# Seven-product units at the start of the second halves' pairs, with their sums prepared in the mixers, and a plain unit's pieces held in program order behind them

## The chip, the cores and the metric

The kernel runs on one core of a Trainium2 chip. The metric is the time of the device for one execution in microseconds; 2365.54 us is the median of three runs (2365.01 to 2366.05).

## The reference

Two layers act on 256 tokens of width D = 2048, in float32. Layer 0 mixes tokens with a bidirectional mLSTM, layer 1 with a bidirectional HGRN2 recurrence; each mixer is followed by a gated MLP with a width-3 depthwise convolution, and a last RMSNorm closes the trunk. The change touches the matrix products behind the mixers and in the gated MLP:

```python
def conv_glu(hn, w_up, conv_w, conv_b, w_down):
    u = hn @ w_up
    a, v = jnp.split(u, 2, axis=-1)          # each 256 x 5504
    ...
    return (jax.nn.gelu(c, approximate=False) * v) @ w_down

for layer in range(DEPTH):
    ...
    h = h + mix
    h = h + conv_glu(rmsnorm(h, norm_ffn_g[layer]), ...)
return rmsnorm(h, final_g)
```

## The kernel before

**Weights.** All weights stream from HBM in the order of use. Each loaded tile `raw` is split into a high part wh (a cast on ScalarE, L147) and a low part wl (a subtraction on VectorE, L148); activations are split likewise. A product of two blocks is then three matmuls: high by high, high by low, low by high. A generator yields the split pieces (128 x 1024 or 128 x 512) and runs a few pieces ahead of TensorE.

**The gated MLP** of a layer is done in two halves of its inner width, 22 and 21 K-tiles of 128. A half consists of an up phase (L365 and L369, TensorE computes u for its K-tiles, then convolution, gelu and product) and two *pairs*. A pair multiplies the half's K-tiles by two column blocks of 512 of w_down and adds the result into hm, which holds the residual stream. The mixers' output projections have one such pair each, over 16 K-tiles.

**Units.** A pair takes its K-tiles by twos. Such a unit is a product of 2 x 2 by 2 x 2 blocks (two token halves, two K-tiles, two column blocks). A *plain* unit does the eight block products, 24 matmuls of 128x512, into four banks C11 to C22 (named pc in the profile), from two pieces of 1024 columns. A *seven-product* unit does seven products, 21 matmuls, partly into four other banks P1, P6, P7, P5 (named mm), with differences of weights and of activations as operands. It needs pieces of 1024, 1024, 1024 and 512 columns. Its activation sums sx are made by `token_sums` (L579 to L581) in the up phase. Its weight sums come from VectorE in one of two ways: *on the fly* in `combine` (four subtractions, L207), or *prepared*: `prepare` loads the unit's 1 MB, makes four subtractions of 128x512 (L646) and stores 1 MB to a scratch area in HBM, tscr; the pair later loads 768 KB of weights plus 1 MB of prepared blocks in place of 1 MB of weights. Preparation goes on in the mixers (through SyncE's queue, loads with L403, stores with L649) and in the up phases (through POOL's queue, L407). After the last seven-product unit of a pair, `mid` (L593 to L604) adds the banks P1 to P5 into hm: a ScalarE copy L596, VectorE adds L597 to L602, POOL adds L603 and L604. At a pair's end `done` (L610) adds the C banks.

**The tables.** SEVEN names the seven-product units of each layer's halves, FLY those made on the fly, FIRST how many of the first half's first pair are prepared in the mixer, SPLIT how the second pair of the second half is shared between mixer, first up phase and second up phase. `prepare_early` is given the start and the period of the preparation in the mixer.

**Order.** Operations are written by the generators and then put in order for each engine by a scheduler, with the exception of those that are wrapped in `pin` (kept in the order of the program). Side jobs such as `prepare` and `token_sums` are stepped by a clock of estimated costs.

**The end.** The last pair's last three units are done token half by token half (`ending`, L245 to L270). In the second token half the block C22 is computed in two parts of 256 columns, the latter into a bank named rest. `FinalNorm.half` (L515 to L544) adds the banks, squares, sums, takes the power on POOL (L534), scales and stores.

## Time and profile before

| | |
|---|---|
| median of 3 runs | 2365.54 us |
| profiled execution | 2365.45 us, its span 2363.7 us |
| TensorE busy | 2352.0 us (100%) |
| VectorE busy | 2012.2 us (85%) |
| ScalarE busy | 1478.2 us (63%) |
| POOL busy | 309.1 us (13%) |
| DMA | 656.06 MB, mean 278 GB/s |
| chain that ended last | TensorE 98%, VectorE 1% |
| granted TensorE clock | 0.999 of full speed |

The page's span runs from the first to the last instruction. Its times are microseconds. In a timeline a row begins with its start and its length; xN joins N instructions; what stands in brackets is the idle time ahead of it and what ended it. "pc<-wh,g" is a matmul that writes bank pc from weights wh and activations g. TensorE's matmuls are pipelined, so that the modelled end of one lies behind the start of the next. The halves of layer 0's MLP have their pairs at about 634 to 742 us and 974 to 1080 us, those of layer 1 at about 1910 to 2018 us and 2250 to 2356 us.

### The profile page before, as it was taken

The numbers are of one execution on the slowest core, as the hardware profiler recorded it, in microseconds if no ns is written. First come the engines' busy times: TensorE is split into PE (matmuls) and PEld (weight loads), VectorE is DVE, ScalarE is ACT, GpSimd is POOL, SyncE is SP. The second block draws the span as 40 slices with busy tenths as digits, with TensorE's granted clock in tenths as the row PEclk, the third lists the DMA queues.
The fourth block names the chain that finished last, engine by engine and source line by source line (L and its number), as shares of the span: only waits on it lengthen the run. The fifth ranks groups of instructions, "written<-read, shape, count | busy, mean of one in ns | idle before, by whom it ended". The sixth has DMA issues, their size and how long they took to land.

```text
span 2363.7 us, 38636 instructions
## 1 busy us (share of the span) xinstructions
PE 2352.0 (100%) x14533; PEld 2013.4 (85%) x14533; DVE 2012.2 (85%) x3123; ACT 1478.2 (63%) x2352; POOL 309.1 (13%) x460
## 2 busy tenths in 40 slices
PE   9999999999999999999999999999999999999998
PEld 7888888888888888888888888888888888888887
DVE  7777787999998999897888788788799989899888
ACT  7655456555665555676777777766555577555565
POOL 0100001111000111000232322220011100111100
PEclk9999999999999999999999999999999999999999
DMA  8776756899898999886656666566799999799985
GB/s 303 239 245 244 239 204 216 292 337 338 308 358 312 311 334 332 290 316 228 212 203 222 214 220 209 206 207 234 247 329 338 319 336 362 272 332 327 333 328 205
DMA packets 129180, 656.06 MB, mean 278 GB/s; under 512 B 14544, under 2 KB 15696, under 8 KB 85600
## 3 DMA queue, kind: packets, MB, share of 16 engines
q1 hardware_dynamic: 96192, 536.32, 64.3%
q0 software_dynamic: 32224, 116.47, 13.8%
q8 instruction: 114, 1.87, 0.3%
q10 hardware_dynamic: 576, 0.79, 0.1%
q14 instruction: 74, 0.61, 0.1%
HBM read 576.92 MB, written 76.61 MB: 276 GB/s over the span
## 4 chain that ended last, share of the span: by engine, by line
PE 98%; DVE 1%; issue 0%; DMA 0%; ACT 0%; POOL 0%; SPq 0%; POOLq 0%; DVEq 0%
PE mm L365 37%; PE mm L369 19%; PE mm L381 18%; PE pc L236 11%; PE mm L236 9%; PE pn L865 1%; PE py L1124 1%; DVE wl L148 0%; PE pd L1074 0%; PE pa L1074 0%; PE pz L446 0%; DMA raw<-in_w_first 0%; PE S L851 0%; PE pz L1145 0%; PE pa L1099 0%
## 5 line engine op out<-in xcount | busy, mean ns | idle before, releaser
L365 PE MATMUL mm<-xt,wh 128*128 128x512 f32 x3776 | 1312.6, 394 | 0.2 <-issue 0.2
L148 DVE TENSOR_TENSOR wl<-raw,wh 128x1024 fp32r<-128x1024 f32 (+1 forms) x844 | 1034.2, 1232 | 230.4 <-ACT wh L147 223.2
L147 ACT CAST wh<-raw 128x1024 fp32r<-128x1024 f32 (+1 forms) x844 | 874.9, 1043 | 545.5 <-PE mm L365 346.6
L369 PE MATMUL mm<-xt,wl 128*128 128x256 f32 x3776 | 1043.6, 278 | 0.0
L365 PEld LDWEIGHTS mm<-xt,wh 128*128 128x128 f32 x3776 | 705.7, 188 | 160.9 <-issue 0.4
L369 PEld LDWEIGHTS mm<-xt,wl 128*128 128x128 f32 x3776 | 709.5, 188 | 4.8 <-issue 0.3
L381 PE MATMUL mm<-wh,xt 128*128 128x512 f32 x1024 | 324.1, 392 | 1.6 <-ACT wh L147 1.5
L236 PE MATMUL pc<-wh,g 128*128 128x512 f32 (+1 forms) x676 | 231.6, 388 | 0.0
L381 PEld LDWEIGHTS mm<-wh,xt 128*128 128x128 f32 x1024 | 190.9, 188 | 41.0 <-ACT wh L147 2.1
L646 DVE TENSOR_TENSOR praw<-praw 128x512 f32<-128x512 f32 x284 | 196.4, 692 | 14.6 <-DMA praw<-in_w_d 9.0
L381 PE MATMUL mm<-wl,xt 128*128 128x512 f32 x512 | 199.7, 391 | 0.0
L236 PE MATMUL mm<-wh,sx 128*128 128x512 f32 x456 | 160.1, 389 | 0.0
L147 ACT CAST wh<-T 128x512 fp32r<-128x512 f32 (+1 forms) x152 | 124.5, 835 | 46.8 <-PE pc L236 19.5
L148 DVE TENSOR_TENSOR wl<-T,wh 128x1024 fp32r<-128x1024 f32 (+1 forms) x152 | 142.4, 959 | 12.5 <-ACT wh L147 11.9
L236 PEld LDWEIGHTS pc<-wh,g 128*128 128x128 f32 x676 | 126.7, 188 | 25.9
L236 PE MATMUL pc<-wl,g 128*128 128x512 f32 (+1 forms) x338 | 131.5, 389 | 0.6 <-DVE wl L148 0.5
L1214 ACT COPY avc<-mm 128x256 f32<-128x256 f32 x172 | 64.3, 374 | 87.9 <-PE mm L369 87.9
L381 PEld LDWEIGHTS mm<-wl,xt 128*128 128x128 f32 x512 | 96.2, 188 | 18.6
L407 POOL DMA_DIRECT2D praw<-in_w_d x108 | 57.7, 535 | 413.0 <-DMA tscr<-praw 408.4
L1087 DVE TENSOR_TENSOR QK<-QK,G 128x256 f32<-128x256 f32 x224 | 104.6, 515 | 5.0 <-ACT kq L1066 4.7
L236 PEld LDWEIGHTS mm<-wh,sx 128*128 128x128 f32 x456 | 85.6, 188 | 17.8
L1066 ACT COPY kq<-QK 128x512 f32<-128x512 f32 x112 | 74.5, 670 | 41.2 <-DVE QK L1087 35.1
(248 smaller groups left out, 2337.5 us busy)
## 6 DMA issues: line engine op xcount, KB each, us to landing
raw<-in_w_up SPq DMA_DIRECT2D x172, 1024.0 KB, 7.7
praw<-in_w_d POOLq DMA_DIRECT2D x108, 512.0 KB, 6.8
tscr<-praw POOLq DMA_DIRECT2D x108, 512.0 KB, 8.7
T<-tscr SPq DMA_DIRECT2D x71, 768.0 KB, 7.2
raw<-in_w_d SPq DMA_DIRECT2D x68, 768.0 KB, 6.7
raw<-in_w_bq SPq DMA_DIRECT2D x48, 1024.0 KB, 5.0
raw<-in_w_ao SPq DMA_DIRECT2D x24, 1024.0 KB, 4.8
raw<-tscr SPq DMA_DIRECT2D x71, 256.0 KB, 7.0
```

Of the source, the lines that this page charges most:

```text
L147: pin(act.copy(wh[:, :m], r))
L148: pin(dve.tensor_tensor(wl[:, :m], r, wh[:, :m].bitcast(F32), ALU.subtract))
L236: pin(pe.matmul(ps, a, b, start=bank not in begun, stop=stop and i == 2))
L365: hold(pe.matmul(ps[f], wh[:, c:c + P], x, start=k + kk == 0, stop=False))
L369: hold(pe.matmul(ps[f][:, 0:T], wl[:, c:c + P], x[:, 0:T], start=False, stop=k + kk == ch.nk - 1))
L381: pe.matmul(ps[t], x[:, a + t * P:a + (t + 1) * P], w[:, c], start=st and i == 0, stop=sp and i == 2)
L407: tc.keep_in_program_order(pool.dma_start(dst, src))
L646: hold(dve.tensor_tensor(out, x, y, ALU.subtract))
L865: pe.matmul(pn[:, 0:258], w, v, start=(i == 0), stop=(i == len(parts) - 1))
L1066: act.copy(m, blocks(QK, h))
L1087: dve.tensor_tensor(two[:, j], two[:, j], by[:, j], ALU.mult)
L1214: act.copy(z, p[:, T:2 * T])
```

## The change

Both pairs of both second halves get unit 0 as a seven-product unit (layer 0: units 0 to 8 for 1 to 8; layer 1: 0 to 7 for 1 to 7). Layer 0's unit 5 is made on the fly in the second half's first pair only, and prepared in its second pair. Of the first halves' first pairs, nine and ten units are prepared in the mixers instead of seven; the second pair's shares are (0, 3, 6) and (0, 4, 4) instead of (0, 1, 6) twice. So 12 and 13 units are prepared in the mixers for 10 and 10, 14 and 14 in the first up phases as before, 14 and 12 in the second for 13 and 13. The mixers' preparation starts sooner and steps faster. The pieces of a plain unit right behind a seven-product unit are held in program order, as are `mid`'s first copy and first add. In the final norm, the add of C22 takes 256 columns in the second token half.

```diff
@@ -47,10 +47,10 @@
 LEAD = 48
 TEMP = 3
 GATES = 4 * AH
-SEVEN = (range(10), range(1, 9)), (range(10), range(1, 8))
-FLY = (), (5,), (), ()
-FIRST = 7
-SPLIT = (0, 1, 6), (0, 1, 6)
+SEVEN = (range(10), range(9)), (range(10), range(8))
+FLY = ((), ()), ((5,), ()), ((), ()), ((), ())
+FIRST = 9, 10
+SPLIT = (0, 3, 6), (0, 4, 4)
 END = 3
 SCRATCH = 4096
 SEVEN_MIX = (2, 4, 6)
@@ -209,13 +209,14 @@
 
         for u in range(units):
             r = raw(u)
-            yield *parts(r[:, 0:1024], 1024, more=ch.pool), 1
+            hold = pin if u - 1 in ch.seven and u not in ch.seven else lambda ins: ins
+            yield *parts(r[:, 0:1024], 1024, hold, ch.pool), 1
             if u + 1 in ch.seven and u + 1 not in ch.stored:
                 combine(u + 1)
             if u in ch.seven:
                 yield *parts(kept[u][:, 0:1024], 1024, more=ch.pool), 1
             if 2 * u + 1 < ch.nk:
-                yield *parts(r[:, 1024:2048], 1024, more=ch.pool), 1
+                yield *parts(r[:, 1024:2048], 1024, hold, ch.pool), 1
             if u in ch.seven:
                 yield *parts(kept[u][:, 1024:1536], 512, more=ch.pool), 1
 
@@ -274,6 +275,7 @@
         alone = max(set(range(units)) - set(ch.seven))
         for u in range(units):
             if ch.last and u == units - END:
+                assert id(C22) not in begun
                 ending(u)
                 held.pop()
                 return
@@ -522,8 +524,8 @@
             dve.tensor_scalar(rc, ss[:, 2:3], 1.0 / D, rc, ALU.mult, ALU.add)
             last = keep.tile([P, 512], F32, tag=f"xt{4 + t}", name="fl")
             h = hm[:, t, 1536:2048]
-            dve.tensor_tensor(h, h, ps[1], ALU.add)
             m = 256 if t else 512
+            dve.tensor_tensor(h[:, 0:m], h[:, 0:m], ps[1][:, 0:m], ALU.add)
             dve.scalar_tensor_tensor(last[:, 0:m], h[:, 0:m], 1.0 / D, h[:, 0:m], ALU.mult, ALU.mult, accum_out=ss[:, 3:4])
             dve.tensor_tensor(rc, rc, ss[:, 3:4], ALU.add)
             if t:
@@ -593,8 +595,8 @@
         def mid(ps):
             P1, P6, P7, P5 = ps
             u = ev.tile([P, 512], F32, tag="jk", bufs=1, name="u")
-            act.copy(u, P1)
-            dve.tensor_tensor(part(0, 0), part(0, 0), P1, ALU.add)
+            pin(act.copy(u, P1))
+            pin(dve.tensor_tensor(part(0, 0), part(0, 0), P1, ALU.add))
             dve.tensor_tensor(u, u, P6, ALU.add)
             dve.tensor_tensor(part(0, 1), part(0, 1), P5, ALU.add)
             dve.tensor_tensor(part(0, 1), part(0, 1), u, ALU.add)
@@ -947,7 +949,7 @@
                 norm.finish()
                 done_v(ps, note)
                 side.push(start(gs))
-                prepare_early(box["mp"], 0, 62.0, 25.0)
+                prepare_early(box["mp"], 0, 55.0, 19.0)
 
             last = {}
 
@@ -992,7 +994,7 @@
             mp = box["mp"] = stack.enter_context(tc.tile_pool(name="hg", bufs=1))
             box["lv"] = mp.tile([P, 2 * P], F32, name="lv")
             late(box["lv"][:, 0:FINE * QUAD], cst_d[:, C_LV:])
-            prepare_early(mp, 1, 30.0, 38.0)
+            prepare_early(mp, 1, 30.0, 27.0)
             box["turn"] = 0
             lb = box["lb"] = mp.tile([P, KT], F32, name="lb")
             oml = box["oml"] = mp.tile([P, KT], F32, name="oml")
@@ -1284,9 +1286,10 @@
 
             w0, w1 = w_d0[layer][:, f0 * 1024:(f0 + nf) * 1024], w_d3[layer] if part else w_d1[layer]
             fly = FLY[2 * layer + part]
-            n = len(seven) - len(fly)
-            chunks.append(two(w0, 0, nxt if part else None, seven, fly, (0, 0, n) if part else (FIRST, n - FIRST)))
-            chunks.append(two(w1, 2, nxt if part and not ending else None, seven, fly, SPLIT[layer] if part else (0, n)))
+            m, n = (len(seven) - len(f) for f in fly)
+            early_ = FIRST[layer]
+            chunks.append(two(w0, 0, nxt if part else None, seven, fly[0], (0, 0, m) if part else (early_, m - early_)))
+            chunks.append(two(w1, 2, nxt if part and not ending else None, seven, fly[1], SPLIT[layer] if part else (0, n)))
             if part:
                 chunks[-1].last = ending
                 if ending:
```

TensorE, at the start of the second half's first pair in layer 0, before (mm at L369 ends the up phase; g are activations, sx their sums):

```order
L369 MATMUL mm<-xt_3941,wl 128x256
L236 MATMUL pc<-wh,g_7398 128x512
L236 MATMUL pc<-wl,g_7398 128x512
L236 MATMUL pc<-wh,g_7398 128x512
L236 MATMUL pc<-wh,g_7506 128x512
L236 MATMUL pc<-wl,g_7506 128x512
```

and in the change:

```order
L371 MATMUL mm<-xt_3961,wl 128x256
L237 MATMUL mm<-wh,g_7418 128x512
L237 MATMUL mm<-wl,g_7418 128x512
L237 MATMUL mm<-wh,g_7418 128x512
L237 MATMUL pc<-wh,g_7418 128x512
L237 MATMUL pc<-wl,g_7418 128x512
L237 MATMUL pc<-wh,g_7418 128x512
L237 MATMUL mm<-wh,sx 128x512
```

The pair begins with the first product of a seven-product unit, into an mm bank, and not with the first of a plain one. Over the whole program the matmuls into pc fall by 60 and those into mm rise by 48.

VectorE at the end of the first half's second pair in layer 0, before:

```order
L148 TENSOR_TENSOR wl<-T,wh 128x512
L597 TENSOR_TENSOR hm<-hm,mm 128x512
L599 TENSOR_TENSOR hm<-hm,mm 128x512
L601 TENSOR_TENSOR hm<-hm,mm 128x512
L148 TENSOR_TENSOR wl<-raw,wh 128x1024
L598 TENSOR_TENSOR u<-u,mm 128x512
L148 TENSOR_TENSOR wl<-raw,wh 128x1024 x2
```

and in the change (its lines 599, 600, 601, 603 are lines 597, 598, 599, 601 of before):

```order
L148 TENSOR_TENSOR wl<-T,wh 128x512
L601 TENSOR_TENSOR hm<-hm,mm 128x512
L148 TENSOR_TENSOR wl<-raw,wh 128x1024
L603 TENSOR_TENSOR hm<-hm,mm 128x512
L148 TENSOR_TENSOR wl<-raw,wh 128x1024 x2
L599 TENSOR_TENSOR hm<-hm,mm 128x512
L600 TENSOR_TENSOR u<-u,mm 128x512
```

The rows "wl<-raw" are the plain unit 10's two pieces and then the next phase's first. The pieces moved ahead of three of the four adds.

VectorE at the very end, second token half, before:

```order
L525 TENSOR_TENSOR hm<-hm,pc 128x512
L522 TENSOR_SCALAR fss<-fss 128x1
L527 SCALAR_TENSOR_TENSOR fl,fss<-hm 128x256
L528 TENSOR_TENSOR fss<-fss 128x1
L531 TENSOR_TENSOR hm<-hm,rest 128x256
L532 SCALAR_TENSOR_TENSOR fl,fss<-hm 128x256
L533 TENSOR_TENSOR fss<-fss 128x1
```

and in the change (lines 524, 528, 529, 530, 533, 534, 535 are 522, 525, 527, 528, 531, 532, 533 of before):

```order
L524 TENSOR_SCALAR fss<-fss 128x1
L528 TENSOR_TENSOR hm<-hm,pc 128x256
L533 TENSOR_TENSOR hm<-hm,rest 128x256
L529 SCALAR_TENSOR_TENSOR fl,fss<-hm 128x256
L534 SCALAR_TENSOR_TENSOR fl,fss<-hm 128x256
L530 TENSOR_TENSOR fss<-fss 128x1
L535 TENSOR_TENSOR fss<-fss 128x1
```

The add of rest, which needs the last matmul, moved ahead of the first part's square and its sum.

## The prediction

> **What bounds the kernel now.** I read the page's first part, then the chain of waits, then TensorE's waits.
>
> ```profile
> PE 2352.0 (100%) x14533; PEld 2013.4 (85%) x14533; DVE 2012.2 (85%) x3123; ACT 1478.2 (63%) x2352; POOL 309.1 (13%) x460
> PE 98%; DVE 1%; issue 0%; DMA 0%; ACT 0%; POOL 0%; SPq 0%; POOLq 0%; DVEq 0%
> 974.81 5.45 PE pc L236 x24
> 323.20 10.88 PE pc L236 x48
> PE mm L381 <- ACT wh L147: 1.5, 2, 0.9
> PE pc L236 <- DVE wl L148: 0.8, 3, 0.3
> ```
>
> TensorE is busy for 2352.0 of 2363.7 us and carries 98% of the chain that ended last. So the time can fall in three ways only: fewer matmuls, fewer of the short waits in front of them, or a shorter end after the last one. VectorE at 85% is next; it makes the low halves (wl, L148) that TensorE reads, and its two waits of this kind are visible above. The profiled execution took 2365.45 us; the median of the runs shown is 2365.54, 0.09 above, and I add that at the end. What a measurement can tell from no change, 0.2%, is 4.73 us.
>
> **Twelve matmuls fewer.** Four pairs of column blocks get a seven-product unit where a plain one was: 7 products of 3 matmuls for 8 of 3, so 3 fewer each, 12 in all. The price of one is its spacing, not its duration. The two chain rows above give it: 24 matmuls in 5.45 us and 48 in 10.88, 0.227 us each. The mean duration of the same form stands in this group row:
>
> ```profile
> L236 PE MATMUL mm<-wh,sx 128*128 128x512 f32 x456 | 160.1, 389 | 0.0
> ```
>
> 389 ns is longer because neighbours overlap; by it twelve would be 4.67 us, the far bound. I take 12 x 0.227 = **-2.72**. The Trainium skill, page "TensorE: Matmul & The Clock Gate", section "Back-to-back issue gap", gives about 131 ns as the sustained spacing of matmuls with 512 columns; by it the twelve would be an estimated 1.57 us and the forecast 1.15 us later. The chain rows disagree with that page for this kernel's float32 operands (0.227), and I stay with the rows.
>
> **Two waits behind a seven-product unit.** At the end of each first half, second pair, plain unit 10 follows seven-product unit 9. TensorE and VectorE in layer 0, from the timeline:
>
> ```profile
> 732.81 0.69 DVE L597 TENSOR_TENSOR hm<-hm,mm 128x512 f32<-128x512 f32 x1 [0.94 <-ACT u L596]
> 734.17 0.69 DVE L599 TENSOR_TENSOR hm<-hm,mm 128x512 f32<-128x512 f32 x1 [0.68 <-PE mm L236]
> 734.78 0.68 DVE L601 TENSOR_TENSOR hm<-hm,mm 128x512 f32<-128x512 f32 x1
> 735.11 1.29 PE L236 MATMUL pc<-wh,g 128*128 128x512 f32 x5
> 735.37 1.22 DVE L148 TENSOR_TENSOR wl<-raw,wh 128x1024 fp32r<-128x1024 f32 x1
> 736.51 0.68 DVE L598 TENSOR_TENSOR u<-u,mm 128x512 f32<-128x512 f32 x1
> 736.65 0.50 PE L236 MATMUL pc<-wl,g 128*128 128x512 f32 x1 [0.25 <-DVE wl L148]
> 736.99 0.63 PE L236 MATMUL pc<-wh,g 128*128 128x512 f32 x2
> ...
> 737.68 0.63 PE L236 MATMUL pc<-wh,g 128*128 128x512 f32 x2
> 738.38 0.50 PE L236 MATMUL pc<-wl,g 128*128 128x512 f32 x1
> 738.72 0.39 PE L236 MATMUL pc<-wh,g 128*128 128x512 f32 x1
> ```
>
> Five matmuls from 735.11 should let the sixth start at 736.24; it starts at 736.65 (0.41 lost) and the next 0.34 later instead of 0.227 (0.11). Two from 737.68 should end at 738.13; the next starts at 738.38 (0.25), and the one after loses 0.11 again: 0.87 together. The cause is VectorE's order: L599 waits for TensorE, L601 follows it, and only then come unit 10's pieces. Layer 1 repeats it:
>
> ```profile
> 2011.14 1.29 PE L236 MATMUL pc<-wh,g 128*128 128x512 f32 x5
> 2012.68 0.50 PE L236 MATMUL pc<-wl,g 128*128 128x512 f32 x1 [0.25 <-DVE wl L148]
> ...
> 2013.71 0.63 PE L236 MATMUL pc<-wh,g 128*128 128x512 f32 x2
> 2014.41 0.50 PE L236 MATMUL pc<-wl,g 128*128 128x512 f32 x1
> ```
>
> In the change both pieces are held, and one add (layer 0) or none (layer 1) stands ahead of the first. Layer 0 by the durations above: the add may start 0.42 after the start of product P5's last matmul (733.75 to 734.17); add pitch 0.61 (734.17 to 734.78), piece pitch 1.14 (735.37 to 736.51). First piece ready at 0.42 + 0.61 + 1.14 = 2.2; TensorE needs it 14 matmuls later, 3.2. Second: 2.2 + 0.61 + 1.14 = 3.9 against 20 matmuls, 4.5. Both waits go: 2 x 0.87 = **-1.74**. Lower bound 0, if each only moves to the next piece. What is late instead are the adds L597 and L598; nobody needs them before the banks are reused, some 35 matmuls on.
>
> **The second halves' first units.** A seven-product unit wants pieces of 1024, 1024, 1024 and 512 columns from VectorE instead of two of 1024: 1.14 + 0.61 = 1.74 us more per pair, while TensorE takes 3 x 0.227 = 0.68 less. So each of the four pair starts presses VectorE by 2.42 us. The busy times by window (length, busy PE, PEld, DVE, ACT, POOL with counts, clock, DMA share, GB/s) are the first pairs of layer 0's halves, its second half's second pair, and layer 1's:
>
> ```profile
> 634.00:690.00 56.00, 56.00 (x250) 46.38 (x250) 51.10 (x57) 42.27 (x52) 3.54 (x2) 1.00 0.89 342
> 974.00:1028.00 54.00, 54.00 (x241) 44.51 (x240) 49.33 (x58) 38.53 (x47) 3.46 (x2) 1.00 0.85 308
> 1028.00:1080.00 52.00, 52.00 (x239) 43.09 (x237) 48.47 (x54) 37.76 (x50) 2.57 (x2) 1.00 0.70 240
> 2250.00:2300.00 50.00, 50.00 (x224) 41.46 (x223) 42.94 (x50) 34.00 (x42) 3.47 (x2) 1.00 0.90 330
> 984.00:994.00 10.00, 10.00 (x46) 8.29 (x45) 10.00 (x12) 7.33 (x8) 0.00 (x0) 1.00 0.72 238
> ```
>
> Layer 0's first half already begins with a seven-product unit and TensorE is busy for 56.00 of its 56.00 us, so the cheap bound is 0. Its second half is fuller: 984 to 994 VectorE is busy all the time (unit 5's sums are made on the fly there). The first pair goes from 49.33 to 51.07 of 53.3 us, 96%; the second from 48.47 + 1.74, less four on-the-fly subtractions of 0.61, to 47.8 of 51.3, 93%; layer 1 to 44.7 of 49.3. The dear bound is all four pressures uncovered, 4 x 2.42 = 9.68. I take **+0.4**, a sixth of one, nearest to the 56.00 row.
>
> The sums themselves are made earlier. Five more units are prepared in the mixers (two in layer 0, three in layer 1): 4 subtractions each, 20 on VectorE, and 2 MB of loads and stores each through SP's queue. Beside them lies this:
>
> ```profile
> 220.00:322.00 102.00, 102.00 (x520) 86.71 (x519) 76.33 (x141) 56.32 (x96) 2.92 (x4) 1.00 0.68 231
> 1400.00:1500.00 100.00, 100.00 (x781) 86.17 (x780) 85.77 (x142) 72.78 (x136) 32.11 (x43) 1.00 0.61 213
> SPq L649 <- DVE praw L646: 43.3, 24, 5.9
> ```
>
> VectorE has 14 to 25% free, DMA a third, so I cost them at nothing. If the cover were gone, 20 x 0.61 = 12 us would be on the path. SP's stores (L649) wait for the subtractions, 43.3 us in 24 waits, and the loads of weights queue behind them: ten more stores, 18 us more of such waiting, covered while those loads stay three tiles ahead. A stored unit reads 768 KB more: 2.5 us at the 308 GB/s of its window, of which DMA has 15% free.
>
> **The end.** The last token half's final operations:
>
> ```profile
> 2354.93 0.42 DVE L527 SCALAR_TENSOR_TENSOR fl<-hm 128x256 f32<-128x256 f32 x1
> 2355.39 0.16 DVE L528 TENSOR_TENSOR fss<-fss 128x1 f32<-128x1 f32 x1
> 2355.48 0.28 PE L236 MATMUL rest<-wh,g 128*128 128x256 f32 x1
> 2355.79 0.42 DVE L531 TENSOR_TENSOR hm<-hm,rest 128x256 f32<-128x256 f32 x1 [0.25 <-PE rest L236]
> 2356.25 0.43 DVE L532 SCALAR_TENSOR_TENSOR fl<-hm 128x256 f32<-128x256 f32 x1
> 2356.72 0.16 DVE L533 TENSOR_TENSOR fss<-fss 128x1 f32<-128x1 f32 x1
> 2356.96 0.56 POOL L534 TENSOR_TENSOR fss<-fss,mhalf 128x1 f32<-128x1 f32 x1 [4.89 <-DVE fss L533]
> ```
>
> L527 and L528 now run before TensorE's last matmul, in time that is idle anyway. In the change they stand behind L531, which waits for that matmul. Their pitch, 0.46 (2354.93 to 2355.39) and 0.17, comes onto the path: **+0.63**. The add of C22, halved to 256 columns, saves nothing, as VectorE waits after it. Bounds: 0, if the sum is ready sooner than I think, and 0.8.
>
> **Places where only the order moved.** Between the layers an added L610 stands ahead of a piece and the operations that make xt, for which TensorE waited there already; one more add is 0.61, some of it under existing waiting: **+0.4**. In layer 1's mixer output a wait for wl (the third in the 0.8 us above) meets nine matmuls brought forward, 2 us of cover against 1.14 + 0.6 us of extra work: **-0.3**. Bounds for the two together: -1 and +1.
>
> Sum: 2365.45 - 2.72 - 1.74 + 0.40 + 0.63 + 0.40 - 0.30 = 2362.12, and with 0.09 **2362.2**. Own range 2360.9 to 2363.5, the small terms each halved or doubled.
>
> **Rivals.**
>
> - VectorE becomes the bound where second halves begin. For it: 10.00 of 10 us busy. Against it: the first half's 56.00. It decides when the pieces' lead at a pair's start is under 2.42 us. In all four pairs it costs 9.68 for my 0.4: 2371.5, slower (0.07). In layer 0's two alone, 4.84: 2366.6 (0.09).
> - The held pieces do not remove the waits: the add that stands ahead of them still waits for TensorE, or the pieces behind them come late by as much. Then 1.74 stays: 2363.9 (0.14).
> - More goes than I think: the pinned adds cost nothing at the end or between the layers, and VectorE is never late. Without the three added costs 2362.2 - 1.43 = 2360.8; with the 4.67 us of the mean duration as well, 2358.8. Faster (0.18), mostly close to the line.
>
> **How the numbers follow.** Mine has 0.52. Faster by over 0.2% is below 2360.8: 0.19, the last rival and a little of mine. Slower is above 2370.3: 0.07. The rest, 0.74, is within. The range of 8 in 10 goes from 2359.8 to 2365.4: below it lies part of the last rival, above it VectorE as the bound.
>
> **What would show it.** In the changed profile: 12 fewer L237 matmuls and 2.7 us less busy TensorE; no wait for wl near 733 and 2009; TensorE unbroken in the first 20 us of each second half; POOL's last power 2.1 us after the start of the last matmul instead of 1.48. Gaps behind L148 at the start of a second half would make the slower rival right; a wait for wl at 736 that remains, the second; a time under 2361, the third.

## The result

The changed kernel takes 2376.42 us (median of six runs, 2375.7 to 2377.81) against 2365.6 for the kernel before on the same chip: a ratio of 1.0047, 95% interval 1.0035 to 1.0058. It is slower by 10.8 us. The forecast was 2362.2, with 0.07 for slower, and the range ended at 2365.4.

The page of the changed kernel (busy times and the chain of waits), whose profiled execution took 2376.27 us with a span of 2374.5:

```profile
PE 2354.7 (99%) x14521; PEld 2011.6 (85%) x14521; DVE 2026.1 (85%) x3159; ACT 1484.7 (63%) x2364; POOL 311.4 (13%) x460
PE 93%; DVE 3%; DMA 2%; issue 1%; ACT 1%; POOL 0%; SPq 0%; POOLq 0%; DVEq 0%; ACTq 0%
```

There are twelve matmuls fewer, as planned, but TensorE's share of the chain fell from 98% to 93%: VectorE, DMA and "issue" (the engine waited for nothing that the profile shows) stand in it now. TensorE's waits (us in total, times, longest) name the places:

```profile
PE pd L1076 <- issue: 3.1, 1, 3.1
PE mm L237 <- DVE wl L148: 2.4, 6, 0.6
PE mm L383 <- ACT wh L147: 2.1, 2, 1.3
PE pc L237 <- ACT wh L147: 1.0, 2, 0.8
```

Where the time went is seen best by stage. Both views below count only the line of the pairs' matmuls (L236 before, L237 after), in windows from the start of a stage's first such matmul to the start of its last: layer 0's first half and second half, layer 1's mixer up to its output (with the boundary between the layers at its start), that output, layer 1's first half and second half. Before:

```profile
634.60:741.50 106.90, 106.56 (x468) 87.47 (x468) 1.00 0.88 333
974.60:1079.40 104.80, 103.93 (x455) 85.24 (x456) 1.00 0.78 276
1079.40:1596.70 517.30, 0.42 (x2) 0.00 (x1) 1.00 0.63 215
1596.70:1640.30 43.60, 42.03 (x182) 34.05 (x183) 1.00 0.69 240
1910.70:2017.50 106.80, 106.48 (x468) 87.42 (x468) 1.00 0.87 333
2250.70:2355.50 104.80, 104.80 (x477) 87.39 (x477) 1.00 0.74 268
```

After:

```profile
635.20:742.80 107.60, 107.02 (x467) 87.25 (x468) 1.00 0.90 331
976.00:1079.40 103.40, 102.55 (x449) 84.08 (x450) 1.00 0.83 304
1079.40:1603.10 523.70, 0.41 (x3) 0.04 (x1) 1.00 0.65 225
1603.10:1648.50 45.40, 42.68 (x182) 33.93 (x183) 1.00 0.66 229
1918.80:2028.00 109.20, 107.77 (x467) 87.03 (x468) 1.00 0.89 329
2261.20:2365.90 104.70, 104.33 (x471) 85.97 (x471) 1.00 0.76 277
```

The first column after the window is its length. Read down the two lists: +0.7, -1.4, +6.4, +1.8, +2.4, -0.1. With 0.6 at the program's start and 0.4 behind the last matmul (8.2 to 8.6) that is 10.8, the whole difference of the spans; the up phases between them stayed equal to 0.1. (The 0.6 are waits for the first weights, the row of L383 above: 2.1 us here, 1.5 before.) So the first halves' pairs, where two waits were to go, became longer, and the largest loss lies in layer 1's mixer, whose matmuls the change does not touch.

**The mixer: TensorE waits for its own program.** TensorE in the changed kernel, from the timeline:

```profile
1378.46 0.82 PE L1076 MATMUL pd<-kq 128*32 128x32 f32 x72
1382.39 0.26 PE L1076 MATMUL pd<-kq 128*32 128x32 f32 x6 [3.10 <-issue]
...
1383.60 0.63 PE L383 MATMUL mm<-wl,xt 128*128 128x512 f32 x1
1384.03 1.05 PE L383 MATMUL mm<-wh,xt 128*128 128x512 f32 x2
```

In the middle of a group of 78 equal small matmuls TensorE stops for 3.10 us and no semaphore is the reason ("issue"). Then eight large matmuls run at about 0.43 us each instead of 0.227. The granted clock of that stretch is the 0.53 in this row of the windows (us, busy with count, clock, DMA share, GB/s); from 1382.6 to 1385.9 alone it is 0.50:

```profile
1382.40:1386.00 3.60, 3.60 (x14) 0.53 0.95 237
```

What it stopped for stands in the DMA view, where instructions have a queue of their own. First the whole program, then the window 1379.9 to 1382.3:

```profile
q8 instruction: 114, 1.87, 0.3%
...
q8 instruction: 1, 0.02, 2.5%
```

114 packets carry 1.87 MB, 16.4 KB each. The queue does not name its engine; if it is TensorE's, then 2 x 14521 matmuls and weight loads make one packet for 255 of its instructions, and the times below fit that. A whole group of these small matmuls is 128 with as many loads, so it uses up a packet's worth, and in the kernel before it takes 1.2 us (1380.3 to 1381.5). In the ten microseconds from 1370 to 1379.9 no packet of this queue ran, with the data queue busy 74% of the time; the packet came at 1380.0, after TensorE had stopped, and TensorE went on at 1382.39. In the kernel before, the packet ahead of the same group (1380.3 to 1381.5 there) came between 1370 and 1377, and nothing stopped. The changed kernel has a second stop of this kind, 0.60 us at 1532.7, 2.3 us after a packet at 1530.4.

**The pairs: VectorE's pieces come late.** VectorE, POOL and TensorE at the start of the second pair of layer 0's first half, in the changed kernel:

```profile
694.30 1.30 POOL L605 TENSOR_TENSOR hm<-hm,u 128x512 f32<-128x512 f32 x1 [79.86 <-PE pc L237]
694.66 5.39 DVE L148 TENSOR_TENSOR wl<-raw,wh 128x1024 fp32r<-128x1024 f32 x3
695.57 2.26 POOL L606 TENSOR_TENSOR hm<-hm,u 128x512 f32<-128x512 f32 x1
698.97 0.50 PE L237 MATMUL mm<-wl,g 128*128 128x512 f32 x1 [0.58 <-DVE wl L148]
```

And the same operations before:

```profile
686.08 1.29 POOL L603 TENSOR_TENSOR hm<-hm,u 128x512 f32<-128x512 f32 x1 [72.21 <-DVE u L602]
686.50 1.95 DVE L148 TENSOR_TENSOR wl<-raw,wh 128x1024 fp32r<-128x1024 f32 x1
687.34 2.28 POOL L604 TENSOR_TENSOR hm<-hm,u 128x512 f32<-128x512 f32 x1
688.97 1.73 DVE L148 TENSOR_TENSOR wl<-raw,wh 128x1024 fp32r<-128x1024 f32 x1
```

The last of `mid`'s adds, and POOL's two behind it, come 8 us later, in the units that the second pair begins with; that the holds at the end of the first pair do this, the run with the holds alone shows below. Of the three pieces joined in the second row, the two beside POOL's adds take 2.02 and 2.31 us, and the third, which begins after POOL's last add has ended at 697.83, takes 1.21. Before, two pieces were slow in the same way (1.95 and 1.73), but they were not followed directly by a third, and TensorE did not wait. In layer 1 the same stands at 1976 to 1984.

### The profile page after: what moved, and what is told of

Its sections match the earlier page's. It is cut to its first block, busy times and chain, and to the rows that moved or that the text cites. A ratio compares the mean times of both kernels' runs of the same rounds, so it can differ in the third digit from the quotient of the medians.

```text
span 2374.5 us, 38715 instructions
## 1 busy us (share of the span) xinstructions
PE 2354.7 (99%) x14521; PEld 2011.6 (85%) x14521; DVE 2026.1 (85%) x3159; ACT 1484.7 (63%) x2364; POOL 311.4 (13%) x460
## 3 DMA queue, kind: packets, MB, share of 16 engines
q8 instruction: 114, 1.87, 0.3%
## 4 chain that ended last, share of the span: by engine, by line
PE 93%; DVE 3%; DMA 2%; issue 1%; ACT 1%; POOL 0%; SPq 0%; POOLq 0%; DVEq 0%; ACTq 0%
PE mm L367 37%; PE mm L371 18%; PE mm L383 18%; PE pc L237 8%; PE mm L237 7%; DVE wl L148 2%; DMA raw<-in_w_d 1%; PE pn L867 1%; PE py L1126 1%; PE pd L1076 1%; ACT wh L147 0%; PE pa L1076 0%; PE pz L448 0%; DMA T<-tscr 0%; DMA raw<-in_w_first 0%
## 5 line engine op out<-in xcount | busy, mean ns | idle before, releaser
L383 PE MATMUL mm<-wh,xt 128*128 128x512 f32 x1024 | 324.2, 393 | 2.2 <-ACT wh L147 2.1
L648 DVE TENSOR_TENSOR praw<-praw 128x512 f32<-128x512 f32 x304 | 209.1, 688 | 24.5 <-DMA praw<-in_w_d 15.1
L383 PEld LDWEIGHTS mm<-wh,xt 128*128 128x128 f32 x1024 | 191.8, 189 | 41.8 <-ACT wh L147 2.7
L237 PE MATMUL pc<-wh,g 128*128 128x512 f32 (+1 forms) x636 | 219.7, 388 | 0.0
L383 PE MATMUL mm<-wl,xt 128*128 128x512 f32 x512 | 200.4, 392 | 0.0
L237 PE MATMUL mm<-wh,sx 128*128 128x512 f32 x480 | 166.6, 390 | 0.0
L148 DVE TENSOR_TENSOR wl<-T,wh 128x512 fp32r<-128x512 f32 (+1 forms) x160 | 151.0, 966 | 16.6 <-ACT wh L147 16.2
L147 ACT CAST wh<-T 128x512 fp32r<-128x512 f32 (+1 forms) x160 | 130.5, 835 | 46.1 <-DMA T<-tscr 16.2
L237 PEld LDWEIGHTS pc<-wh,g 128*128 128x128 f32 x636 | 119.1, 188 | 24.6 <-ACT wh L147 0.2
L237 PE MATMUL pc<-wl,g 128*128 128x512 f32 (+1 forms) x318 | 123.7, 389 | 0.0
L383 PEld LDWEIGHTS mm<-wl,xt 128*128 128x128 f32 x512 | 96.6, 189 | 18.7
L237 PEld LDWEIGHTS mm<-wh,sx 128*128 128x128 f32 x480 | 90.0, 188 | 19.0 <-ACT wh L147 0.3
L409 POOL DMA_DIRECT2D tscr<-praw x108 | 58.1, 538 | 351.4 <-DVE praw L648 225.9
```

Of the source, the lines that this page charges most:

```text
L147: pin(act.copy(wh[:, :m], r))
L148: pin(dve.tensor_tensor(wl[:, :m], r, wh[:, :m].bitcast(F32), ALU.subtract))
L237: pin(pe.matmul(ps, a, b, start=bank not in begun, stop=stop and i == 2))
L383: pe.matmul(ps[t], x[:, a + t * P:a + (t + 1) * P], w[:, c], start=st and i == 0, stop=sp and i == 2)
L409: tc.keep_in_program_order(pool.dma_start(dst, src))
L648: hold(dve.tensor_tensor(out, x, y, ALU.subtract))
```

## The experiments

**Holds taken out of the changed kernel:**

```diff
-            hold = pin if u - 1 in ch.seven and u not in ch.seven else lambda ins: ins
+            hold = lambda ins: ins
-            pin(act.copy(u, P1))
-            pin(dve.tensor_tensor(part(0, 0), part(0, 0), P1, ALU.add))
+            act.copy(u, P1)
+            dve.tensor_tensor(part(0, 0), part(0, 0), P1, ALU.add)
```

> The change without its program-order holds (pieces of plain units behind seven-product units, and the first copy and add after the last seven-product unit, are free again). Theory A: the holds push the adds after a pair's last seven-product unit, and with them POOL's two adds, 8 us later, into the next pair's first units, where VectorE then falls behind. Then the waits at 692 to 699 us (1.4) and 1976 to 1985 us (2.4) go, the two old waits of 0.87 each come back, net about -2: some 2374.3, with the mixer stall at 1382 still there. Rival B: the extra seven-product units and sums alone load VectorE; then the waits in the second pairs of the first halves stay and the time is the changed kernel's 2376.4 or 1.7 more.

2371.79 us (2368.81 to 2375.02), ratio to before 1.0026 (1.0016 to 1.0037). The window of the last two pairs, and the stop in the mixer:

```profile
2255.60:2359.10 103.50, 103.46 (x471) 86.37 (x471) 1.00 0.76 282
...
1381.13 0.27 PE L1076 MATMUL pd<-kq 128*32 128x32 f32 x7 [3.06 <-issue]
```

Without holds the mixer's output takes 43.9 again (45.4 in the change, 43.6 before), and the last two pairs take 103.5: the six matmuls do come off in layer 1. The old waits at 737 are back. The stop in the mixer stayed, so the holds don't cause it. Layer 1's first half still takes 108.2 us (109.2 in the change, 106.8 before), with a wait of 1.06 us for wl at 1975.5: part of the loss there is not the holds'. The gain of 4.6 is more than the 2 that were expected. In the profiled execution, one of the shorter of the eight (2369.48), the clock stays at 1.00 behind the stop. Over all eight the mean granted clock is 0.998 in four (2371.56 to 2375.02) and 0.999 in four (2368.81 to 2372.01), while in the changed kernel it is 0.997 or 0.998 in all six: so the slow clock behind the stop seems to come in some executions only.

**Layer 1's mixer prepares ten units at the old pace**, the rest of the changed kernel as it is:

```diff
-FIRST = 9, 10
-SPLIT = (0, 3, 6), (0, 4, 4)
+FIRST = 9, 7
+SPLIT = (0, 3, 6), (0, 1, 7)
-            prepare_early(mp, 1, 30.0, 27.0)
+            prepare_early(mp, 1, 30.0, 38.0)
```

> The change with layer 1's mixer preparing 10 units at period 38 as before (seven for the first half's first pair; the second pair of its second half shares 0, 1, 7), all else as changed. Theory C: 7.8 us of the 10.8 are lost in layer 1's mixer, because three more units' loads and stores, at a shorter period, delay TensorE's instruction fetches and its last pieces; then the mixer takes 588.5 us again from its first matmul (1081) to the first up matmul, and the time is about 2368.7. Rival D: the loss there is an accident of where the instruction blocks end, not of the preparation; then it may stay anywhere between 0 and 7.8.

2371.84 us, ratio 1.0030 (1.0019 to 1.0041): 4.6 less than the change. The mixer up to its output is back to 519.4 from 523.7 (517.3 before). The 3.1 us stop is gone; two shorter ones of 0.9 us each, at 1156 and 1404, are there. So such stops come with the old preparation of this mixer too. And the run changes two things: with the preparation the scheduler's order changes, and the group of small matmuls near 1380 stands 26 instructions further on in TensorE's program (16799 matmuls and loads ahead of it in the trace, for 16773). It does not tell less preparation from another place.

**The changed kernel's 13 units at the old pace:**

```diff
-            prepare_early(mp, 1, 30.0, 27.0)
+            prepare_early(mp, 1, 30.0, 38.0)
```

> The change with layer 1's mixer still preparing 13 units, but at period 38 instead of 27. Theory C1 (crowding): transfers spread out, no fetch is 10 us late, the stall of 3.3 us at 1382 and the slow clock behind it (1.9) go: about 2371. Theory C2 (the number of units): nothing changes, 2376.4. Both leave the waits of the halves.

2391.77 us, ratio 1.0111 (1.0094 to 1.0128). Neither theory's number: 13 steps of 38 us from 30 on end at 524, and the mixer up to its output takes 517 to 524, so the last units are prepared in one go at its end. The output takes 60.1 us for 43.6, and TensorE waits for ScalarE and VectorE there:

```profile
PE mm L237 <- ACT wh L147: 3.5, 1, 3.5
PE mm L383 <- DVE yb L390: 3.2, 1, 3.2
```

So more units need the faster pace. Up to there the mixer runs as in the kernel above: the same two stops (0.98 and 0.89 us, at 1157 and 1405), none at 1382, and the group of small matmuls at the same place (16799). For the stop it adds nothing to that run.

**Only the place in the instruction packets moved.** The change with 106 idle matmuls at the program's start for 90, narrower so that they take about as long; the order of all else is the same, and every later instruction of TensorE stands further on. In the trace each of these matmuls is two, with a load each (212 for 180), so the shift is 64 instructions, and not the 32 of the expectation.

```diff
-    for i in range(90):
+    for i in range(106):
-        pe.matmul(idle[o:o + QUAD, 0:53], ones[:, 0:QUAD], ones[:, 0:53], start=True, stop=True)
+        pe.matmul(idle[o:o + QUAD, 0:45], ones[:, 0:QUAD], ones[:, 0:45], start=True, stop=True)
```

> The change with 106 idle matmuls of 45 columns at the start instead of 90 of 53; the order of everything else is the same, but TensorE's instruction stream is shifted by 32 instructions. Rival D (alignment): the run of 256 small matmul instructions at 1378 to 1382 us begins 44 instead of 13 instructions behind a multiple of 256 (with the same offset), its next block is asked for 3 to 4 us sooner, and the stall of 3.3 us with its 1.9 us of slow clock goes, perhaps to come in another place: about 2371. Theory C (preparation alone decides): 2376.4.

2372.24 us (2370.34 to 2373.32), ratio 1.0029 (1.0018 to 1.0041): 4.2 less than the change, although the pairs begin 1.1 us later and layer 0's second up phase is 1.7 us longer (a wait for wl at 956 among others). The mixer up to its output takes 517.5, for 523.7 in the change and 517.3 before; the second stop is gone too. The instruction packet ahead of the same group of small matmuls (now at 1380.69) came 11 us before it, in the window 1366 to 1370:

```profile
q8 instruction: 1, 0.02, 1.8%
```

Nothing was taken from VectorE, from the queues of data or from the preparation, and yet the stop and the slow clock behind it went. So the 4.7 us (3.1 stopped, 8 x 0.2 at the lower clock) are shown to come from the supply of instructions, and with them nearly all of the 6.4 us by which the mixer had grown.

**The kernel before with such a shift**, 72 idle matmuls of 66 columns for 90 of 53:

```diff
-    for i in range(90):
+    for i in range(72):
-        pe.matmul(idle[o:o + QUAD, 0:53], ones[:, 0:QUAD], ones[:, 0:53], start=True, stop=True)
+        pe.matmul(idle[o:o + QUAD, 0:66], ones[:, 0:QUAD], ones[:, 0:66], start=True, stop=True)
```

> The kernel before with 72 idle matmuls of 66 columns in place of 90 of 53, the order of all else the same: TensorE's instruction stream is 36 instructions earlier, and its run of 256 small matmul instructions near 1380 us begins where the changed kernel's does, 13 instructions behind a block's end. Theory D (where the blocks end decides): a stall of about 3 us there, with slow clock behind it 5: 2368 to 2370.5. Theory C (the added preparation's transfers are needed too): no stall or a small one, 2365.1 to 2366.

2365.79 us, ratio 1.0004 (0.9995 to 1.0014), and no stop at the group of small matmuls where the changed kernel has its own; one of 0.4 us at 1357, where the kernel before has none. This does not bring the group to the changed kernel's place, as was meant: the shift is 72 instructions and not 36, and 16739 matmuls and loads stand ahead of the group, for 16773 in the changed kernel and 16811 in the kernel before. So the changed kernel's place with the old preparation was not run. What the run shows is that a shift alone can bring a small stop.

**The changed kernel with neither the holds nor the old place**: the first diff and that of the 106 idle matmuls together.

```diff
-            hold = pin if u - 1 in ch.seven and u not in ch.seven else lambda ins: ins
+            hold = lambda ins: ins
...
-    for i in range(90):
+    for i in range(106):
```

> The change without holds and with the 32 instructions' shift: what is left is the added units and the sums made in the mixers. Theory A with D: the stall of 3.2 us at 1381 of the run without holds goes, and with it its spread of 6 us between executions: 2366 to 2368, of which layer 1's first half is 1.4. Rival: the spread and the loss come from the added transfers: 2371.8 with the same spread.

2367.2 us (2365.78 to 2367.57), ratio 1.0011 (1.0002 to 1.0020): 4.6 less than without the shift, and the stop at 1381 is gone, and with it the spread: 1.8 us between the executions for 6.2. It is still above the kernel before, though twelve matmuls are gone: the pairs begin 1.9 us later, layer 1's first half takes 108.4 us for 106.8, and the second halves give 1.3 and 0.9 back. The idle stretch itself is not what makes the pairs late: the first matmul behind it starts at 5.22 us, before at 5.42. The 1.9 us come between 80 and 135 us, in layer 0's mixer, in all three kernels with more idle matmuls, and their cause stays open.

**The holds alone**, in the kernel before:

```diff
-            yield *parts(r[:, 0:1024], 1024, more=ch.pool), 1
+            hold = pin if u - 1 in ch.seven and u not in ch.seven else lambda ins: ins
+            yield *parts(r[:, 0:1024], 1024, hold, ch.pool), 1
...
-            act.copy(u, P1)
-            dve.tensor_tensor(part(0, 0), part(0, 0), P1, ALU.add)
+            pin(act.copy(u, P1))
+            pin(dve.tensor_tensor(part(0, 0), part(0, 0), P1, ALU.add))
```

> The kernel before with the change's holds alone (a plain unit's pieces behind a seven-product unit and the first copy and add after the last one, in all pairs), no other unit. Theory A: the two old waits go (-1.74), but the later adds stall the second pairs of both first halves (1.6 and some 2) and the held pieces in layer 1's mixer output cost 1.4: about 2368.4. Rival B (the holds are harmless, the units and sums do the damage): 2363.4.

2370.57 us (2369.57 to 2372.24), ratio 1.0027 (1.0017 to 1.0037), 5.8 us more than the kernel before. Layer 0's and layer 1's first halves and the mixer's output, and the wait between the layers:

```profile
635.20:742.80 107.60, 107.02 (x467) 87.27 (x468) 1.00 0.89 332
1601.20:1646.20 45.00, 42.67 (x183) 33.88 (x183) 1.00 0.64 230
1916.50:2024.20 107.70, 107.08 (x468) 87.30 (x468) 1.00 0.89 332
...
PE pz L447 <- DVE hm L611: 2.2, 2, 1.3
```

Without one matmul or sum changed, 107.6, 45.0 and 107.7 stand where before there were 106.9, 43.6 and 106.8. In the change they were 107.6, 45.4 and 109.2: layer 0's loss is here whole, the output's for the most part, and of layer 1's first half 0.9 of 2.4. To this come 2.2 us of waits between the layers, where displaced adds stand before what TensorE needs, and slow clock behind them:

```profile
1085.30:1088.70 3.40, 3.40 (x9) 2.65 (x9) 2.33 (x8) 3.37 (x8) 0.00 (x0) 0.50 1.00 419
```

TensorE is busy throughout; the last columns are the clock, 0.50, DMA share and GB/s. The profiled execution is the longest of the eight (2372.24), and the mean granted clock is 0.998 in three of them and 0.999 in five, so the slow clock does not seem to come in all. The changed kernel has waits of only 0.4 us there and full clock. The waits at 736 and 2012 are gone, and cost less than what came for them.

**POOL's two adds given to VectorE**, in the kernel with the holds alone:

```diff
-            pool.tensor_tensor(part(1, 0), part(1, 0), u, ALU.add)
-            pool.tensor_tensor(part(1, 1), part(1, 1), u, ALU.add)
+            dve.tensor_tensor(part(1, 0), part(1, 0), u, ALU.add)
+            dve.tensor_tensor(part(1, 1), part(1, 1), u, ALU.add)
```

> Edit: the kernel before with the holds of the change everywhere (as the earlier run with the holds alone, 2370.57), and the two adds that GpSimd has in the middle of each pair given to VectorE. Theory (VectorE's pieces take 1.8 instead of 1.2 us while GpSimd's two adds run beside them, and these adds were moved by the holds into the first units of the next pair): the pieces at 692 to 699 and 1976 to 1985 take 1.2 to 1.3 us, the stalls of 0.5 to 0.8 us there shrink or go, and the time falls 1 to 3 us under 2370.57, to 2367.5 to 2369.5, although VectorE has two adds of 0.61 us more in each of twelve pairs. Rival (VectorE's own added time counts and not the neighbour): the pieces come 1.2 us later by the two adds, the stalls stay or grow, and the time is 2370.5 to 2374.

2370.87 us, ratio 1.0025 (1.0015 to 1.0036): the time is the same as with the holds alone. By place both theories are right in part. VectorE at the place of the late pieces, and layer 0's first half:

```profile
694.37 2.34 DVE L148 TENSOR_TENSOR wl<-raw,wh 128x1024 fp32r<-128x1024 f32 x2
696.64 0.67 DVE L604 TENSOR_TENSOR hm<-hm,u 128x512 f32<-128x512 f32 x1
697.24 0.68 DVE L605 TENSOR_TENSOR hm<-hm,u 128x512 f32<-128x512 f32 x1
...
634.90:741.60 106.70, 106.69 (x467) 87.36 (x468) 1.00 0.91 342
```

With POOL idle a piece takes 1.21 us, where two took 2.02 and 2.31; the three with both adds between them take 4.68 us (694.37 to 699.05) instead of 5.39, and the stalls at 699 and 1980 are gone: the first halves take 106.7 us each, 0.9 and 1.0 less. Between the layers, where nothing covers them, the two adds stand on VectorE ahead of the operations that make xt, and TensorE waits 3.1 us there for 2.2; the half clock follows here too. So POOL's adds make the pieces late, and giving the work to VectorE moves the loss. That the adds cost less on VectorE than beside it agrees with the Trainium skill, page "SBUF — State Buffer", section "Who interferes with whom": a VectorE operation with two inputs in SBUF contends with a GpSimd (POOL) operation that reads there. For such a pair the section gives no duration; here a piece takes 2.02 and 2.31 us for 1.21.

**Holds only where a wait was to be removed**: in the kernel before, in the last pair of each first half, with `mid`'s copy and its first four adds kept behind the held pieces (`keep_`).

```diff
-            yield *parts(r[:, 0:1024], 1024, more=ch.pool), 1
+            hold = pin if ch.hold and u - 1 in ch.seven and u not in ch.seven else lambda ins: ins
+            yield *parts(r[:, 0:1024], 1024, hold, ch.pool), 1
...
+            keep_ = pin if ch.hold else lambda ins: ins
-            act.copy(u, P1)
+            keep_(act.copy(u, P1))
...
+            chunks[-1].hold = not part
```

> Edit: the kernel before with one thing of the change, put where only the last pair of a layer's first half has it: there the plain unit's two pieces behind seven-product unit 9 keep their place in program order, and of the four adds and the copy that follow the middle of the pair all stand behind the held pieces. TensorE's instructions and the preparation in the mixers are as in the kernel before; 20 of VectorE's operations stand elsewhere. Theory 1 (the waits were worth what the prediction said, and the cost of the holds in the study that had them everywhere came from the adds that they moved into the next pair's first units, the layer boundary and the mixer's output): the waits of 0.87 us at 735 to 739 and at 2012 to 2015 go and nothing comes instead, so 1.74 us less than before, about 2363.0 (2362 to 2364 by the median). Rival (what is held always pushes something else late: pieces that are held move the same VectorE time to the first units of the next pair): waits of 0.5 to 0.8 us at 690 to 700 and 1975 to 1985 come as with the holds everywhere, and the time is not below the time before, 2364.8 to 2367.

2363.29 us (median of eleven, 2362.35 to 2364.69) against 2365.2, 1.9 less where 1.74 was expected; the ratio is 0.9993, with an interval of 0.9984 to 1.0002 that just touches 1. VectorE at the place of the first wait, and the two first halves:

```profile
731.77 3.49 DVE L148 TENSOR_TENSOR wl<-raw,wh 128x1024 fp32r<-128x1024 f32 x3 [0.44 <-ACT wh L147]
735.18 0.68 DVE L599 TENSOR_TENSOR hm<-hm,mm 128x512 f32<-128x512 f32 x1
...
634.10:740.00 105.90, 105.90 (x467) 87.64 (x468) 1.00 0.89 340
1908.40:2014.40 106.00, 105.96 (x468) 87.67 (x468) 1.00 0.89 340
```

The pieces go first and the adds follow. TensorE is busy all of the 105.9 us: 1.0 and 0.8 us less than before. An up phase comes next, and the displaced adds cost nothing in it. The two windows carry the reading here; the times alone leave the gain at the edge of the noise.

**Layer 0's part of the change alone**, in the kernel before, with holds in the first halves' last pairs (only `mid`'s copy and first add behind them) and 96 idle matmuls:

```diff
-SEVEN = (range(10), range(1, 9)), (range(10), range(1, 8))
+SEVEN = (range(10), range(9)), (range(10), range(1, 8))
-FIRST = 7
-SPLIT = (0, 1, 6), (0, 1, 6)
+FIRST = 9, 7
+SPLIT = (0, 3, 6), (0, 1, 6)
...
-                prepare_early(box["mp"], 0, 62.0, 25.0)
+                prepare_early(box["mp"], 0, 55.0, 19.0)
...
+            chunks[-1].hold = not part
```

> Half of the change: layer 0's second half begins with seven-product units (its sums shared as in the change), layer 1 and the end as before; holds only in the first halves' second pairs, behind which no pair follows; 96 idle matmuls of 50 columns, so that the dense runs of matmuls stand at the same place of their instruction block as before. Six matmuls fewer (-1.36), two waits gone (-1.74), +0.3 at the boundary of the layers: about 2362.4. If the extra units or sums cost something by themselves: 2364 or more.

2366.27 us, ratio 1.0007 (0.9998 to 1.0016). That is 3.9 above the 2362.4 that were expected. Layer 0's last two pairs take 103.4 for 104.8, and the mixer of layer 1 had no stop. But the pairs begin 1.8 us later (lost in layer 0's mixer, as in the two other kernels with more idle matmuls), and layer 1's first half, whose units are unchanged, takes 108.0 for 106.8: the scheduler put `mid`'s adds 5 us later there (POOL's from 1962.1 to 1966.9), and TensorE waits 1.1 us for a piece at 1971.

**Layer 1's part**, on the kernel with the confined holds: both of its last pairs begin with a seven-product unit, and the mixer prepares eleven units, one every 34 us. (Layer 0's unit 5 is prepared for its last pair too, instead of made on the fly.)

```diff
-SEVEN = (range(10), range(1, 9)), (range(10), range(1, 8))
-FIRST = 7
-SPLIT = (0, 1, 6), (0, 1, 6)
+SEVEN = (range(10), range(1, 9)), (range(10), range(8))
+FIRST = 7, 8
+SPLIT = (0, 1, 7), (0, 2, 6)
-            prepare_early(mp, 1, 30.0, 38.0)
+            prepare_early(mp, 1, 30.0, 34.0)
```

> Edit: the previous kernel of this batch (holds in the first halves' last pairs) and layer 1's part of the change alone: its second half's second pair and first pair begin with a seven-product unit, eleven units instead of ten are prepared in layer 1's mixer, one every 34 us instead of 38; layer 0 is as before. The last add of column block 2 covers 256 columns as in the change. Theory 1 (matmuls saved are worth 0.227 us each wherever preparation does not delay TensorE's instruction blocks): 6 matmuls, 1.36 us, on top of 1.74, so 2361.7 to 2362.5. Theory 2 (any further preparation in the mixer starts a late fetch of instructions): a stall of 1 to 4 us in one of layer 1's dense matmul runs, most likely where the run's end lies near 0.8 of a block of 256, and 2363 to 2367. Rival on the second half (VectorE becomes the bound where the second half begins): stalls behind L148 in the first 20 us after 2250, 1 to 2 us, about 2364.

2367.02 us (2364.86 to 2369.21), ratio 1.0008 (0.9999 to 1.0016): 3.7 more than its parent. The profiled execution is the longest of the eleven (2369.21) and has two waits in the mixer. TensorE, and the instruction queue in the window 1526.6 to 1529.0 (in the 6.6 us before it that queue carried nothing):

```profile
1528.94 0.28 PE L371 MATMUL mm<-xt,wl 128*128 128x256 f32 x1 [2.00 <-issue]
...
q8 instruction: 1, 0.02, 2.4%
```

In its parent the packet behind the same group of small matmuls came 0.9 us after the group's end and nothing stopped; here it came 2.9 us after. The group stands at the same place of TensorE's program in both (19537 matmuls and loads ahead of it), so here it is not the place that differs: one unit more in the mixer, at a step of 34 us, goes with a packet that is 2.0 us later. The other wait, 1.1 us at 1248, is for an operation that VectorE did late, behind subtractions of the preparation.

**Layer 1's part without more preparation**: unit 5 of both last pairs is made on the fly, so that TensorE's and VectorE's order stays that of the kernel with the confined holds up to the last up phase, where one unit's activation sums are added.

```diff
-SEVEN = (range(10), range(1, 9)), (range(10), range(1, 8))
-FLY = (), (5,), (), ()
+SEVEN = (range(10), range(1, 9)), (range(10), range(8))
+FLY = ((), ()), ((5,), (5,)), ((), ()), ((5,), (5,))
```

> Edit: the kernel with holds in the first halves' last pairs (2363.29), and layer 1's part of the change (both pairs of its second half begin with a seven-product unit, six matmuls fewer), but with the sums of unit 5 of both pairs made on the fly instead of prepared, so that the mixers prepare ten units each as before, and every transfer and instruction up to the last up phase's end stands as it stood. Column block 2's last add covers 256 columns as in the change. Theory (the matmuls are worth 0.227 us each, and what cost the change its time was the earlier preparation and the adds that the holds moved): no stall over 1 us in layer 1's mixer, its last two pairs 103.5 to 104.0 us instead of 104.8, and the end 0.0 to 0.4 later behind them; 1.0 to 1.36 us less than 2363.29, about 2362.1 (2361.6 to 2362.8). Rival (VectorE, with 4 subtractions and 1.74 us of pieces more in each of the two pairs, becomes the bound there): stalls behind L148 in the last two pairs of 1 to 5 us in all, 2363.5 to 2367.

2364.01 us (2363.36 to 2365.61), ratio 0.9996 (0.9987 to 1.0006). TensorE stands still for no more than 0.2 us at a time in the mixer, which takes 516.8 us. But the last pair has a new wait:

```profile
2341.43 0.50 PE L237 MATMUL pc<-wl,g 128*128 128x512 f32 x1 [1.46 <-DVE wl L148]
```

It is of the kind that the holds removed elsewhere, so they were put there too:

```diff
-            chunks[-1].hold = not part
+            chunks[-1].hold = not part or ending
```

> Edit: the previous kernel (2364.01), with the hold also in the last pair of all: the plain unit 8 that follows seven-product unit 7 there gets both pieces in program order, and the copy and the adds of the middle stand behind them. Three of VectorE's operations and one of ScalarE's stand elsewhere. Theory (a wait behind a seven-product unit is VectorE's order, and with it gone layer 1's six matmuls show in the time): the wait of 1.6 us for wl at 2341 goes, the last two pairs take 103.4 to 103.8 us instead of 105.5, and the time is 1.6 to 2.0 us less than 2364.01, 2362.0 to 2362.4. Rival (VectorE has no time left there with the subtractions made on the fly, and the wait moves to the next piece): stalls behind L148 of 1 us or more remain between 2335 and 2350, and the time is 2363.4 or more.

2364.49 us (2363.7 to 2369.5), ratio 0.9998 (0.9989 to 1.0007), and a wait of 1.4 us at the same place. The rival is right:

```profile
2339.49 0.68 DVE L604 TENSOR_TENSOR hm<-hm,mm 128x512 f32<-128x512 f32 x1
2340.09 3.48 DVE L148 TENSOR_TENSOR wl<-raw,wh 128x1024 fp32r<-128x1024 f32 x3
...
2248.20:2353.60 105.40, 103.99 (x471) 86.06 (x471) 1.00 0.73 270
```

Unit 8's pieces are ahead of the adds now, and the next ones, behind them, are late instead: with eight subtractions more in the last two pairs VectorE has no lead left when the seven-product units end. Of all kernels run, the one with the confined holds is the fastest, 1.9 us below the kernel before.

## Why the prediction was wrong

- **"VectorE has 14 to 25% free, DMA a third, so I cost them at nothing"** is the step that failed most. The sums did not lack engine time; the step had not listed a resource that they share, the fetch of TensorE's instructions through the DMA engines. The dear bound (12 us, the subtractions on the path) was the wrong mechanism. The price was 6.4 us in layer 1's mixer for the 0 of the step: the 3.1 us stop, 1.6 us of slow clock, the second stop of 0.6 and smaller waits. All but 0.2 of it went with the shift, which leaves the sums as they are. That more preparation makes a packet later at the same place is shown once, by 2.0 us, in layer 1's part; how much of the 3.1 us is the preparation's and how much the place's is not. The row that could have warned was on the page: 114 packets of instructions through the same DMA engines, and groups of small matmuls that use one up in 1.2 us.
- **"Two waits behind a seven-product unit", -1.74**: the waits went, and with the holds confined the kernel is 1.9 us faster. What failed is "nobody needs them before the banks are reused", said of the adds that are late instead. VectorE's order is one line: what the adds displace is the next pair's pieces, and POOL's adds then run beside these. The step costed the holds at the two places where a wait was visible and not in the first pairs, where they apply just as well. With them everywhere the account is +5.8 instead of -1.74 (the slow clock between the layers, which the changed kernel does not have, is in some of these executions).
- **"Twelve matmuls fewer", -2.72**: the price was right. Layer 0's last pairs became 1.4 us shorter (six by 0.227 is 1.36), layer 1's 1.3 without holds. In the changed kernel layer 1 gave it back to two waits for wl, at 2279.7 and 2326.3, that put the next matmul 0.33 and 0.34 late, and other small ones. The mean duration (4.67) is refuted.
- **"The second halves' first units", +0.4**, and both rivals with VectorE as the bound there: layer 0's second half has no wait in its first 20 us, so the pressure cost nothing. VectorE did become the bound in layer 1's last pair once eight subtractions were added to it, which marks where the limit lies.
- **"The end", +0.63**: 0.4. POOL's last power starts 1.77 us after the start of the last matmul, not 2.1, because the add and the two squares follow each other every 0.34 us there and not every 0.46:

```profile
2365.89 0.28 PE L237 MATMUL rest<-wh,g 128*128 128x256 f32 x1
...
2367.66 0.56 POOL L536 TENSOR_TENSOR fss<-fss,mhalf 128x1 f32<-128x1 f32 x1 [3.47 <-DVE fss L535]
```

- **"Places where only the order moved"**: between the layers +0.3 for +0.4. In layer 1's mixer output +1.8 for -0.3, wrong in sign: TensorE waits there for the high part of a held piece, which comes late from ScalarE:

```profile
1622.95 0.73 PE L237 MATMUL pc<-wh,yb 128*128 128x512 f32 x2 [0.82 <-ACT wh L147]
```

The side of the result was covered by one rival alone, VectorE at the second halves' start. Its 2371.5 was short of the result too, and its mechanism did not happen.

Two things stay open. Why a packet of instructions is late in one kernel and not in another was not traced to single transfers: moving the place took the long stop away, small stops of 0.4 and 0.9 us came without more preparation in this mixer, and no run has the changed kernel's place with the old preparation. And of layer 1's first half's 2.4 us the holds alone bring 0.9. Another 1.2 to 1.6 is there in the three kernels that have layer 0's part of the change and no holds in the first pairs (108.0 to 108.4 for 106.8): the scheduler puts `mid`'s adds 5 us later in them, in layer 0's part alone though only distant code differs. Why it does is open.

## What to carry to other kernels

A hold that cures a wait moves other work: apply it at the place of the wait only, and follow what it displaces into the next stage, on the neighbour engines too. Before more DMA is called covered, look for what else uses the queues, the instruction packets among them, above all beside groups of very small matmuls. And cost an edit at every place where its condition holds, not only where the wanted effect is seen.

## What was not expected of the hardware

- TensorE's instructions come in packets of 16.4 KB, about 255 instructions each, through DMA. A late packet stopped TensorE for 3.1 us in the changed kernel and for 2.0 in another, with "issue" as the only trace in the waits; it went on 2.3 to 2.4 us after the packet's start (1380.0 to 1382.39, 1526.7 to 1528.94).
- The granted clock is 1.00 or 0.50 in these traces and changes on a grid of 3.41 us: the changed kernel's full clock lasts from 3.56 to 1382.55 us, 404 times 3.413, and the slow clock that follows until 1385.96, once 3.413. In the runs here it is not the length of a stop that decides, but how long TensorE is busy in one step of the grid, as the table shows (its windows are 3.4 or 3.5 us long). With a busy time under half of the step the next step had half clock, even after a stop of only 2.00 us; the stop of 3.06 us without holds lay across two steps, and the next matmuls ran at 0.227. The Trainium skill, page "TensorE: Matmul & The Clock Gate", section "What's actually happening", has the clock fall after an idle window of about 3.4 us that runs free of the work. The traces agree on the length and on the free run, but the window need not be idle throughout.

| kernel | step of the grid, us | TensorE busy in it, us | clock of the next step |
|---|---|---|---|
| changed kernel, stop of 3.10 | 1379.1 to 1382.6 | 0.40 | 0.50 |
| layer 1's part, stop of 2.00 | 1527.0 to 1530.4 | 1.46 | 0.50 |
| holds alone, waits of 0.95 and 1.28 | 1081.9 to 1085.3 | 1.64 | 0.50 |
| without holds, first part of the stop of 3.06 | 1376.1 to 1379.5 | 1.97 | 1.00 |
| without holds, the rest of it | 1379.5 to 1382.9 | 1.77 | 1.00 |

- VectorE's subtraction of 128x1024 takes 1.21 to 1.22 us alone and 1.73 to 2.31 beside POOL's adds.
